# A second copy of the low part of k per head, so that both score products of a fused attention and convolution block contract over 128 rows

## The chip, the cores and the metric

The kernel runs on one core of a Trainium2 chip. The metric is the device time of one execution in microseconds (us), lower being better. TensorE does the matrix products, VectorE (DVE), ScalarE (ACT) and GpSimd (POOL) the rest, and SyncE (SP) issues nearly all DMA transfers, one after the other in program order.

## The reference

One encoder layer on 1024 tokens of 1024 channels. The input is normalised and multiplied by one wide matrix; its columns feed a convolution branch, an attention branch and a gate for each. The two results are joined, projected, added to the input and normalised again. The part that the change touches is the score of the neighbourhood attention, with 8 heads of 64 channels on a grid of 16 rows by 64 columns:

```
hn = rms_norm(h, ln_g[l])
proj = hn @ w_in[l] + b_in[l]
glu_a, glu_b, z_conv, q, k, v, z_att = jnp.split(proj, cuts, axis=-1)
...
# per row of the grid, window of 8 rows x 16 columns, clamped at borders
s = jnp.einsum("bhwd,bhiwjd->bhwij", q_row, k_win).astype(jnp.float32) * scale
s = s + bias
p = jax.nn.softmax(s.reshape(B, N_HEADS, GRID_W, kh * KW), axis=-1)
return jnp.einsum("bhwij,bhiwjd->bhwd", p, v_win)
```

## The kernel before

**Products in two parts.** Matrix products run in fp32r. To keep accuracy, each operand is split into a high part (the fp32r rounding) and a low part (what is left), and a product is the sum of high x high, low x high and high x low. A projection of 128 channels for 512 tokens is 24 matmuls of 512 columns (8 pieces of the contraction, three products each), in one PSUM bank.

**Scores.** Two heads make a pair, since 128 projected channels hold two heads. For a pair `i`, `query` and `kv` (with `q_out`, `k_out`, `v_out`) project q, k and v. For head `a` of the pair the tile `q[a]` holds 128 rows: the high part of q in 64 of them and its low part in the other 64. The tile `kh[a]` holds the high part of the head's k twice, in rows 0 to 63 and again in rows 64 to 127. So one matmul over 128 rows gives (q high + q low) x k high. The low part of k stands once per pair, in `kl`: 64 rows for each head. The second product, q high x k low, reads only the 64 rows of the head. A head is worked in 4 column blocks of 16 query columns; a block needs two score banks (`HF`, two halves of the query rows), each of one product with `kh` and one with `kl`, over 264 and 288 key columns (the two outer blocks) or 352 and 384 (the two inner ones). There are 32 blocks in all. I number them 0 to 31; blocks 0 to 3 are head 0, blocks 24 to 27 are head 6.

**A block's chain.** Scores (`s`, TensorE), minimum with the bias (`s<-s,bias`, DVE), exponential (`prob`, ACT), transposes (`ptp`, TensorE), high part (`pth`, ACT) and low part (`ptl`, DVE), product with v (`po<-pth,v` and `po<-ptl,v`, TensorE), copy (`os`, ACT), transpose back (`po<-ident,os`, TensorE), and `ytok` (ACT, then DVE). The scores of a block stand one block ahead of its transposes.

**What else runs beside it.** DVE does the depthwise convolution: 150 multiply-adds ("taps", `acc<-glu,dwc,acc`) that later feed a LayerNorm and a pointwise product (`ln`, `lnb`, `pw`, `yt`). TensorE fills the time between the steps of the chain with projections: `pq`, `pk`, `pv` of later pairs, `pz` of the gates. After these come the last gates and the output projection (`out`).

**What sets the order.** Every engine executes in program order. The program is written by a planner (class `Clock`): streams of work are woven together by an estimated clock of the engines, and a stream also waits for buffers. `r_u` counts 16 large buffers of 128x1024 fp32 (tag `u`): the tiles of x, of the convolution, of q, k and v, and others. `kv` takes 3 of them for k (two `kh`, one `kl`) and more for v; `scores` gives them back at the last block of a head. When a stream has to wait for a buffer, other work comes first, so a changed number of buffers changes the order on all engines.

**Copies between halves.** Channels of head 1 of a pair lie in rows 64 to 127, those of head 0 in rows 0 to 63. To have a part in both halves, `copy` moves 64 rows x 512 columns (128 KB) by a DMA on SP's queue. `k_out` does three for each half of the tokens: `kh[1]`'s rows of head 0 into both halves of `kh[0]`, and, when these are read, head 1's rows of `kh[1]` into its other half. The bias tiles of the following blocks (`bias<-row`, line 462) and the weights (`wr<-in_w_in`, line 213) go through the same queue.

Of the kernel before, what the change touches and what calls it, by code (L numbers as in the profile page):

```python
# [32 lines left out]
CH_A, CH_B, CH_ZC, CH_Q, CH_K, CH_V, CH_ZA = 0, 4, 8, 12, 16, 20, 24  # L33
# rows of the small-vector tile
V_LN, V_BIN, V_DWB, V_CLG, V_CLB, V_GNC, V_GNA, V_N = 0, 8, 36, 40, 44, 48, 52, 56
# column blocks of 16 queries: (first 8-column granule, granules, bias class)
BLK = [(0, 3, 0), (1, 4, 1), (3, 4, 1), (5, 3, 2)]
BW = [24, 32, 24]
# row halves: (first key row, key rows)
HF = [(0, 11), (4, 12)]  # L40
# [30 lines left out]
class Ring:  # L71
    """the buffers of a tag, by the time from which each is free"""

# [16 lines left out]
class Clock:  # L90
    """Every engine issues in the order of this program. The work comes as streams, generators that give the
    time from which they can go on; they are woven by a clock of the tensor engine and of the others' queues."""

# [55 lines left out]
def block(ctx: ExitStack, tc: tile.TileContext, x, vecs, w_in, dw_w, pw_w, pw_b, rpb, w_out, final_g, out):  # L149
# [41 lines left out]

# [1 line left out]
    warm = const.tile([P, 1], F32, name="warm")  # L193
# [4 lines left out]

# [1 line left out]
    acc = yp.tile([P, NC4, T], F32, name="acc")  # L200
# [4 lines left out]

    # chunks of the projection in the order of the work: glu, q, k and v, gates of the attention and of the convolution
    of = {"g": (CH_B, CH_A), "q": (CH_Q,), "k": (CH_K, CH_V), "a": (CH_ZA,), "c": (CH_ZC,), "p": ()}
# [73 lines left out]
    def turned(h):  # L281
        """first the banks of several chunks at a time, so that each tile of x is turned as it comes"""
        todo_ = list(range(NK))
        for group in ((("tr", "tr", "s", "s", "o", "ln"),) if h == 0 else ()) + (("tr",), ("s",)) * NK:
            ks, todo_ = todo_[:len(group)], todo_[len(group):]
            pts = []
            for k, tag in zip(ks, group):
                yield from RB[tag].get()
                pts.append((k, tag, bank(tag, f"px{h}_{k}", NB[tag])))
            for j in range(4):  # L290
                t = 4 * h + j
                while t not in x_ready:
                    yield ck.now + 0.1
                if x_ready[t] + ck.HOP > ck.now:
                    yield x_ready[t] + ck.HOP
                for k, tag, pt in pts:
                    ck.tp(pt[:, j * P:(j + 1) * P], xt[t][:, k * P:(k + 1) * P], ident)
                    if j == 3:
                        sl = slice(512 * h, 512 * h + 512)
                        e = ck.act(out=hi[k][:, sl], in_=pt, func=AF.Copy, scale=col(V_LN + k))  # L300
                        ck.spawn(low(h, k, pt, sl, e, RB[tag]), -1)
            yield
        for _ in range(4):
            r_u.put()
# [12 lines left out]
    bias = []  # L317
# [9 lines left out]

# [1 line left out]
    ready = {}  # L329

    def split(raw, whi, wlo, after=None, eng="pool"):
        """hi and lo of a weight; gives the time"""
        t = ck.act(after, out=whi, in_=raw, func=AF.Copy)
# [34 lines left out]
    def proj(w, h, name, order=None, tag="pj"):  # L368
        """one chunk of channels for half of the tokens; order: width of the column blocks
        that become the outer dimension of the tokens"""  # L370
        whi, wlo, wt = w
# [18 lines left out]

# [1 line left out]
    # CLS: first query row, first key row written, key rows, window by the row offsets -4..3  # L392
    CLS = ((0, 0, 8, False), (4, 0, 11, True), (8, 4, 12, True), (12, 8, 8, False))
# [3 lines left out]
    def bias_rows():  # L397
# [20 lines left out]
        r_gz.put()  # L418
        # a window that moves with the column: columns c0..c0+n, bias columns from 7 on
        for t, c0, n in ((0, 8, 8), (1, 0, 16), (2, 0, 9)):  # L420
            w = BW[t]
            for h in range(8):
# [3 lines left out]
                yield ck.now + 0.3  # L426
        # a window at the border
        for t, start, cs in ((0, 0, range(8)), (2, 8, range(9, 16))):
            for c in cs:
                nc.sync.dma_start(out=ab[t][:, c, :, start:start + 16], in_=rp8[:, :, 15 - c:31 - c])  # L430
                yield ck.now + 0.3
        # a row of mask before, and laid out for the query rows
        for t in range(3):
# [31 lines left out]

# [1 line left out]
    # a sigmoid is half of 1 + tanh of the half, and the taps carry the half  # L467
    u, conv_end = [], [0.0] * 8
# [21 lines left out]
    def all_taps():  # L490
        """two chunks in turn, so that a tap need not wait for the one before; the last chunk by halves of the tokens"""
        n = 0
# [45 lines left out]

# [1 line left out]
    pair = {}  # L540
# [16 lines left out]
    def kv(i):  # L557
        bk, bv = col(V_BIN + CH_K + i), col(V_BIN + CH_V + i)
        for _ in range(3):
            yield from r_u.get()  # L560
        wk = yield from weight(CH_K + i)
        kh = [U(f"kh{i}_{a}", F32R) for a in range(2)]
        kl = U(f"kl{i}", F32R)
        pair[i][1:3] = kh, kl
# [22 lines left out]
    def q_out(i, q, pq, sl, bq):  # L587
        """q[0]: hi and lo of the first head; q[1]: lo and hi of the second"""
        tag, r = (("gz", r_gz), ("ul", r_ul))[sl.start > 0]
# [17 lines left out]
    def k_out(i, kh, kl, pk, sl, bk):  # L607
        """kh[a]: hi of a head, twice; kl: lo of both"""
        t = ck.act(out=kh[1][:, sl], in_=pk, func=AF.Identity, bias=bk)
        yield t  # L610
        for half in (B, A):
            copy(kh[0][half, sl], kh[1][A, sl])
        t = ck.dve("scalar_tensor_tensor", t, out=kl[:, sl], in0=pk, scalar=bk, in1=kh[1][:, sl].bitcast(F32),
                   op0=ALU.add, op1=ALU.subtract)
        r_pj.put(t)
        yield max(t, ck.now + 2.8)
        pair[i][4][0].append(ck.now)
        copy(kh[1][A, sl], kh[1][B, sl])
        yield ck.now + 2.8
        pair[i][4][1].append(ck.now)  # L620
# [22 lines left out]
    def group_scale(src, ms, sq, sums=None):  # L643
        """ms: (mean of squares over each 64 + eps * sums^2) ** -0.5; sq is scratch"""
        g = sq.rearrange("p (g d) -> p g d", d=64)
# [12 lines left out]

# [1 line left out]
    def grid(ap):  # L660
# [5 lines left out]
    def scores(n):  # L666
        """S of a block of 16 columns of a head, and its exponentials"""
        i, a, b = blocks[n]
# [3 lines left out]
        head = 2 * i + a  # L672
        half = slice(64 * a, 64 * a + 64)
        khg, klg = grid(kh[a]), grid(kl)
        g0, ng, bt = BLK[b]
# [3 lines left out]
        for hf, (r0, nr) in enumerate(HF):  # L679
# [4 lines left out]
            ck.mm(so, q[a][:, qsl], khg[:, r0:r0 + nr, ks], True, False)  # L684
            ck.mm(so, q[a][half, qsl], klg[half, r0:r0 + nr, ks], False, True)
            sps.append(so)
        if b == 3:
            r_u.put()
            r_u.put()
            if a:  # L690
                r_u.put()
# [26 lines left out]
    def attention():  # L718
        """the scores run a block ahead"""
        yield from scores(0)  # L720
# [90 lines left out]

# [1 line left out]
    pwh, pwl, ln_end, stage = [], [], {}, [0]  # L813
# [22 lines left out]
    def pointwise(t):  # L836
# [35 lines left out]
        yield from r_ul.get()  # L872
        # half: z / 2; silu(z) = z / 2 * (1 + tanh(z / 2))
        th = half_tile("ul", f"th{t}")
# [39 lines left out]

# [1 line left out]
    def y_ready(c, h):  # L916
# [11 lines left out]
    def gated(y, pz, c, h, banks):  # L928
        """y: half of what z = pz + bias gates; silu(z) = z / 2 * (1 + tanh(z / 2))"""
        yield from r_gz.get()  # L930
# [21 lines left out]

# [1 line left out]
    def work(items):  # L954
# [73 lines left out]
    last = {}  # L1028
    # the chunks of the output projection that come last
    LATE = (3, 7)  # L1030
    K_OUT = [k for k in range(NK) if k not in LATE] + list(LATE)

    def final_gates():
        """the last two chunks of gates, k by k: each lets go of its part of the normalised input"""
        ends = (CH_ZC + 3, CH_ZA + 3)
# [27 lines left out]

# [1 line left out]
    def split_y(t):  # L1065
# [57 lines left out]
    def pieces(t):  # L1123
        """columns of the products of a tile; the last ones are short"""
        ends = (0, 512, 768, 1024) if t == NT - 1 else (0, 512, 1024)
        return [slice(a, b) for a, b in zip(ends, ends[1:])]
# [108 lines left out]
```

## Time and profile before

| what | value |
|---|---|
| median of 3 runs | 578.21 us (576.79 to 579.08) |
| span of the profiled execution | 576.6 us |
| TensorE busy | 557.6 us, 97% of the span, 2717 matmuls |
| TensorE's granted clock | 1.00 in nearly all of the span (mean 0.997) |
| DVE busy | 414.7 us, 72% |
| ACT, POOL busy | 259.7 us (45%), 191.7 us (33%) |
| chain that ended last | TensorE 82%, DVE 12% |

The span goes from the first to the last instruction of one profiled execution, and the profile gives no other time for that execution. The median of the runs is 1.6 us above the span. A TensorE that is "busy" may still be waiting inside: a matmul's duration holds the time in which it passes through the array, so durations of neighbours overlap. What tells more is the distance from one matmul's start to the next one's.

### The profile page before, as it was taken

The page shows a single profiled execution, that of the slowest core. Times are in us where ns is not written, and L with a number is a line of the kernel's source. Part 1 is how long each engine was busy: PE and PEld are TensorE (multiplying, and loading weights), DVE is VectorE, ACT ScalarE, POOL GpSimd, SP SyncE. Part 2 cuts the span into 40 slices and gives each one's busy share as a digit, 9 for nine tenths or more (in the row PEclk, how much of TensorE's full clock was granted, in tenths as well). Part 3 has the DMA queues.
Part 4 walks back from the last instruction along what each step waited for, and adds up shares of the span by engine and source line. Part 5 has one row for each costly group of instructions (what it writes and reads, how often), then busy time and mean ns, then how long its engine had stood idle before and what let it go on. Part 6 is the DMA issues. An engine that isn't in the chain of part 4 may idle for free.

```text
span 576.6 us, 7793 instructions
## 1 busy us (share of the span) xinstructions
PE 557.6 (97%) x2717; PEld 448.4 (78%) x2717; DVE 414.7 (72%) x665; ACT 259.7 (45%) x634; POOL 191.7 (33%) x176
## 2 busy tenths in 40 slices
PE   4999999899999999999999999999999999999995
PEld 3688887677878777777777877888888878888885
DVE  4747999999789988996899677756745265464232
ACT  5542221134554155544558455665755354253122
POOL 8413543241222331240524533642523353031121
PEclk9999999999999999999999999999999999999998
DMA  9413546652114422332232230120100580043221
GB/s 331 132 21 82 167 128 220 181 158 80 36 56 110 103 61 72 89 101 71 64 114 80 79 90 17 38 59 18 39 0 8 181 286 0 2 146 135 84 74 73
DMA packets 60410, 54.58 MB, mean 95 GB/s; under 512 B 9597, under 2 KB 51381, under 8 KB 60372
## 3 DMA queue, kind: packets, MB, share of 16 engines
q1 hardware_dynamic: 60302, 54.07, 31.0%
q8 instruction: 21, 0.34, 0.2%
q14 instruction: 17, 0.14, 0.1%
q10 hardware_dynamic: 70, 0.03, 0.0%
HBM read 36.58 MB, written 11.58 MB: 84 GB/s over the span
## 4 chain that ended last, share of the span: by engine, by line
PE 82%; DVE 12%; DMA 1%; ACT 1%; POOL 1%; SPq 1%; issue 1%; POOLq 0%; ACTq 0%; DVEq 0%
PE out L127 15%; PE pz L127 15%; DVE acc L140 10%; PE pv L127 8%; PE pk L127 7%; PE s L127 6%; PE pq L127 5%; PE ptp L131 5%; PE po L127 5%; PE pb L127 4%; PE pw L127 4%; PE pa L127 3%; PE po L131 1%; DMA x<-in_x 1%; PE px L131 1%; DVE x L140 1%
## 5 line engine op out<-in xcount | busy, mean ns | idle before, releaser
L140 DVE SCALAR_TENSOR_TENSOR acc<-glu,dwc,acc 128x512 f32<-128x512 f32 (+25 forms) x150 | 187.6, 1275 | 1.1
L144 POOL TENSOR_TENSOR wl<-wr,wh 128x512 fp32r<-128x512 f32 x56 | 89.1, 1610 | 133.1 <-ACT wh L136 127.9
L127 PE MATMUL pz<-hi,wh 128*128 128x512 f32 x128 | 52.3, 408 | 0.0
L127 PE MATMUL out<-wol,yh 128*128 128x512 f32 (+1 forms) x136 | 51.2, 377 | 0.0
L127 PE MATMUL out<-woh,yl 128*128 128x512 f32 (+1 forms) x136 | 51.2, 376 | 0.0
L127 PE MATMUL out<-woh,yh 128*128 128x512 f32 (+1 forms) x136 | 51.2, 376 | 0.0
L127 PE MATMUL pz<-hi,wl 128*128 128x512 f32 x128 | 50.3, 393 | 0.1
L127 PE MATMUL pz<-lo,wh 128*128 128x512 f32 x128 | 50.1, 391 | 0.0
L136 ACT ACTIVATE pth<-ptp 128x512 fp32r<-128x512 f32 x64 | 32.2, 544 | 32.2 <-PE ptp L131 32.2
L136 ACT ACTIVATE wh<-wr 128x512 fp32r<-128x512 f32 x56 | 32.3, 631 | 27.5 <-DMA wr<-in_w_in 14.2
L140 DVE TENSOR_TENSOR ptl<-ptp,pth 128x512 fp32r<-128x512 f32 x64 | 37.1, 614 | 1.7 <-ACT pth L136 1.3
L144 POOL TENSOR_TENSOR ams<-ams,mhalf 128x8 f32<-128x8 f32 x8 | 15.6, 1948 | 62.1 <-DVE ams L140 62.1
L140 DVE TENSOR_TENSOR xr<-out,xr 128x512 f32<-128x512 f32 (+1 forms) x17 | 11.1, 659 | 34.1 <-PE out L127 29.6
L136 ACT ACTIVATE prob<-s,mx 128x264 f32<-128x264 f32 (+1 forms) x64 | 33.7, 537 | 2.1 <-DVE mx L140 2.1
L131 PE MATMUL ptp<-ident,prob 128*128 128x128 f32 x224 | 32.0, 279 | 0.1
L140 DVE CUSTOM_DVE_ANT_0 s<-s,bias 128x264 f32<-128x264 f32 (+1 forms) x64 | 30.7, 507 | 1.6 <-PE s L127 0.7
L136 ACT ACTIVATE os<-po 128x256 f32<-128x256 f32 x32 | 12.4, 389 | 41.3 <-PE po L127 41.2
L127 PEld LDWEIGHTS out<-woh,yh 128*128 128x128 f32 x136 | 25.6, 188 | 4.8
L127 PEld LDWEIGHTS out<-woh,yl 128*128 128x128 f32 x136 | 25.6, 188 | 4.7
L127 PEld LDWEIGHTS out<-wol,yh 128*128 128x128 f32 x136 | 25.6, 188 | 4.6
L127 PE MATMUL po<-ptl,v 128*128 128x256 f32 x112 | 28.5, 284 | 0.5 <-DVE ptl L140 0.5
L131 PEld LDWEIGHTS ptp<-ident,prob 128*128 128x128 f32 x224 | 24.5, 140 | 5.7 <-issue 2.3
(153 smaller groups left out, 1380.7 us busy)
## 6 DMA issues: line engine op xcount, KB each, us to landing
wr<-in_w_in SPq DMA_DIRECT2D x28, 512.0 KB
x<-in_x SPq DMA_DIRECT2D x8, 512.0 KB
wor<-in_w_out SPq DMA_DIRECT2D x8, 512.0 KB
xr<-in_x SPq DMA_DIRECT2D x8, 512.0 KB
out<-xr SPq DMA_DIRECT2D x16, 256.0 KB
kh<-kh SPq DMA_DIRECT2D x24, 128.0 KB
q<-ql SPq DMA_DIRECT2D x16, 128.0 KB
row<-abn SPq DMA_DIRECT2D x16, 96.0 KB
```

Source lines behind the costliest of these rows:

```text
L127: self.nc.tensor.matmul(out, lhsT=lhsT, rhs=rhs, start=start, stop=stop)
L131: self.nc.tensor.transpose(out=out, in_=in_, identity=identity)
L136: self.nc.scalar.activation(**k)
L140: getattr(self.nc.vector, fn)(**k)
L144: getattr(self.nc.gpsimd, fn)(**k)
```

## The change

`kl` becomes two tiles of 128 rows, one per head, like `kh`: `kl[a]` has the low part of head `a`'s k in both halves. `k_out` writes the low parts of both heads into `kl[1]` as before (one DVE instruction) and copies: head 0's rows into both halves of `kl[0]`, then head 1's rows into the other half of `kl[1]`. That is 3 more copies for each half of the tokens, 24 in the kernel. `scores` uses all 128 rows for the second product too, which adds q low x k low to the sum. `kv` takes 4 buffers of `r_u` for k in place of 3, and each head gives back 3 at its last block (before: 2 at head 0, 3 at head 1).

```
     def kv(i):
         bk, bv = col(V_BIN + CH_K + i), col(V_BIN + CH_V + i)
-        for _ in range(3):
+        for _ in range(4):
             yield from r_u.get()
...
-        kl = U(f"kl{i}", F32R)
+        kl = [U(f"kl{i}_{a}", F32R) for a in range(2)]
...
     def k_out(i, kh, kl, pk, sl, bk):
...
         for half in (B, A):
             copy(kh[0][half, sl], kh[1][A, sl])
-        t = ck.dve("scalar_tensor_tensor", t, out=kl[:, sl], in0=pk, scalar=bk, in1=kh[1][:, sl].bitcast(F32),
+        t = ck.dve("scalar_tensor_tensor", t, out=kl[1][:, sl], in0=pk, scalar=bk, in1=kh[1][:, sl].bitcast(F32),
                    op0=ALU.add, op1=ALU.subtract)
         r_pj.put(t)
-        yield max(t, ck.now + 2.8)
+        yield t
+        for half in (B, A):
+            copy(kl[0][half, sl], kl[1][A, sl])
+        yield ck.now + 2.8
+        copy(kh[1][A, sl], kh[1][B, sl])
         pair[i][4][0].append(ck.now)
-        copy(kh[1][A, sl], kh[1][B, sl])
+        copy(kl[1][A, sl], kl[1][B, sl])
         yield ck.now + 2.8
         pair[i][4][1].append(ck.now)
...
     def scores(n):
...
-        half = slice(64 * a, 64 * a + 64)
-        khg, klg = grid(kh[a]), grid(kl)
+        khg, klg = grid(kh[a]), grid(kl[a])
...
             ck.mm(so, q[a][:, qsl], khg[:, r0:r0 + nr, ks], True, False)
-            ck.mm(so, q[a][half, qsl], klg[half, r0:r0 + nr, ks], False, True)
+            ck.mm(so, q[a][:, qsl], klg[:, r0:r0 + nr, ks], False, True)
             sps.append(so)
         if b == 3:
-            r_u.put()
-            r_u.put()
-            if a:
+            for _ in range(3):
                 r_u.put()
```

All engines keep their instructions apart from these copies, but the planner writes another order from the projections of pair 1 on. Three places matter below.

**SP's queue at the first pair**, between the first half's `kh` copies and the bias loads of the first blocks. Before:

```order
L585 DMA kh_0_935<-kh_1_936 64x512 x2
L448 DMA row_12_983<-abn_881 128x192 x2
L585 DMA kh_1_936<-kh_1_936 64x512
L462 DMA bias_0_147<-row_0_639 64x1x192
L462 DMA bias_0_147<-row_4_658 64x1x264
L585 DMA kh_0_935<-kh_1_936 64x512 x2
L462 DMA bias_1_148<-row_8_686 64x1x288
```

Now:

```order
L448 DMA row_12_984<-abn_881 128x192 x2
L585 DMA kl_0_937<-kl_1_938 64x512 x2
L462 DMA bias_0_147<-row_0_639 64x1x192
L585 DMA kh_1_936<-kh_1_936 64x512
L585 DMA kl_1_938<-kl_1_938 64x512
L462 DMA bias_0_147<-row_4_658 64x1x264
L585 DMA kh_0_935<-kh_1_936 64x512 x2
L462 DMA bias_1_148<-row_8_686 64x1x288
L585 DMA kl_0_937<-kl_1_938 64x512 x2
```

The second half's `kh` copies have three `kl` copies more ahead of them, and the second half's `kl_0` copies stand behind them, still ahead of the first block's last bias loads.

**TensorE in block 20** (head 5, first column block), between the transposes of the probabilities and the product with v. Before, the last transposes and the first of 18 `pk` matmuls; 12 `pw` matmuls follow these, and then `po_0`:

```order
L131 MATMUL ptp_0_2_3014<-ident,prob_0_153 128x128
L131 MATMUL ptp_0_2_3014<-ident,prob_0_155 128x128
L127 MATMUL pk_0_3023<-hi_131,wh_2860 128x512
L127 MATMUL pk_0_3023<-lo_139,wh_2860 128x512
L127 MATMUL pk_0_3023<-hi_131,wl_2861 128x512
```

Now, from the last transposes to the transpose back:

```order
L131 MATMUL ptp_0_2_2973<-ident,prob_0_155 128x128
L127 MATMUL pz_1_2905<-hi_138,wh_2655 128x512
L127 MATMUL pz_1_2905<-lo_146,wh_2655 128x512
L127 MATMUL pz_1_2905<-hi_138,wl_2656 128x512
L131 MATMUL ln_2998<-ident,acc 128x128 x4
L131 MATMUL ln_3010<-ident,acc 128x128 x4
L127 MATMUL po_0_2997<-pth_0_0_2970,v_1_2595 128x256
...
L127 MATMUL po_0_2997<-ptl_0_2_2977,v_1_2595 128x256
L131 MATMUL po_0_2997<-ident,os_0_3028 128x128 x2
```

30 large matmuls have become 3 and 8 small transposes, and nothing is left between the last `po_0` product and the transpose back. In block 21, just behind, 4 `lnb` transposes stand between `ptp` and `po_1`, and 4 between `po_1` and its transpose back; the `pk` of the last pair comes after that.

**TensorE in block 9** (head 2, second column block). Before, 3 `pq` matmuls stood between the last products with v and the transpose back; now none does:

```order
L127 MATMUL po_1_2098<-pth_1_2_2078,v_0_1934 128x256
L127 MATMUL po_1_2098<-ptl_1_2_2079,v_0_1934 128x256
L131 MATMUL po_1_2098<-ident,os_1_2109 128x128 x2
```

On DVE, 92 taps stand between the first score instruction of block 0 and that of block 24 before, and 102 now; the other 58 or 48 lie outside.

## Rows read from the trace of the kernel before

**Rows 1.** The page: busy time by engine, and the chain that ended last.

```profile
PE 557.6 (97%) x2717; PEld 448.4 (78%) x2717; DVE 414.7 (72%) x665; ACT 259.7 (45%) x634; POOL 191.7 (33%) x176
...
PE 82%; DVE 12%; DMA 1%; ACT 1%; POOL 1%; SPq 1%; issue 1%; POOLq 0%; ACTq 0%; DVEq 0%
```

**Rows 2.** Stretches: length, busy us of PE, PEld, DVE, ACT, POOL, clock, DMA, GB/s.

```profile
126.50:344.10 217.60, 217.03 (x1105) 170.60 (x1104) 186.91 (x320) 111.11 (x287) 63.89 (x44) 1.00 0.29 79
344.10:366.00 21.90, 21.90 (x108) 16.61 (x107) 18.45 (x39) 13.91 (x36) 11.48 (x9) 1.00 0.11 33
```

**Rows 3.** Instructions on the tile s: durations min/median/max, starts, forms.

```profile
L127 PE MATMUL s<-kh,q x64: 285/402/448, 126.5 to 433.5; 128*128 128x264 f32 x16, 128*128 128x288 f32 x16, 128*128 128x352 f32 x16, 128*128 128x384 f32 x16
...
L127 PE MATMUL s<-kl,q x64: 382/412/442, 126.7 to 433.9; 64*128 64x264 f32 x16, 64*128 64x288 f32 x16, 64*128 64x352 f32 x16, 64*128 64x384 f32 x16
```

**Rows 4.** Timeline of PE in blocks 11 and 14: start, duration, instruction.

```profile
229.86 0.37 PE L127 MATMUL s<-kh,q 128*128 128x264 f32 x1
...
231.13 0.66 PE L131 MATMUL ptp<-ident,prob 128*128 128x128 f32 x4
...
250.01 0.41 PE L127 MATMUL s<-kh,q 128*128 128x352 f32 x1
250.35 0.43 PE L127 MATMUL s<-kl,q 64*128 64x352 f32 x1
250.71 0.45 PE L127 MATMUL s<-kh,q 128*128 128x384 f32 x1
251.08 0.44 PE L127 MATMUL s<-kl,q 64*128 64x384 f32 x1
251.46 1.09 PE L131 MATMUL ptp<-ident,prob 128*128 128x128 f32 x8
```

**Rows 5.** Timeline of PE: products with v that follow one another.

```profile
254.83 0.28 PE L127 MATMUL po<-pth,v 128*128 128x256 f32 x1
254.95 0.28 PE L127 MATMUL po<-ptl,v 128*128 128x256 f32 x1
255.07 0.41 PE L127 MATMUL pv<-hi,wh 128*128 128x512 f32 x1
```

**Rows 6.** Timeline of PE's weight loads in block 14 and just after.

```profile
250.35 0.18 PEld L127 LDWEIGHTS s<-kl,q 64*128 64x128 f32 x1 [0.17 <-issue]
250.71 0.19 PEld L127 LDWEIGHTS s<-kh,q 128*128 128x128 f32 x1 [0.17 <-issue]
...
254.72 0.19 PEld L127 LDWEIGHTS po<-pth,v 128*128 128x128 f32 x1
```

**Rows 7.** Timeline around block 20, all engines: transposes, low part, product, copy, transpose.

```profile
313.29 0.88 PE L131 MATMUL ptp<-ident,prob 128*128 128x128 f32 x6
...
313.92 0.48 PE L127 MATMUL pk<-hi,wh 128*128 128x512 f32 x1
...
316.00 0.69 DVE L140 TENSOR_TENSOR ul<-xn,uh 128x512 fp32r<-128x512 f32 x1
...
316.61 1.01 DVE L140 TENSOR_TENSOR ptl<-ptp,pth 128x512 fp32r<-128x512 f32 x2
...
321.41 0.28 PE L127 MATMUL po<-ptl,v 128*128 128x256 f32 x1
...
322.23 0.38 PE L131 MATMUL po<-ident,os 128*128 128x128 f32 x2
```

**Rows 8.** Timeline of SP's queue at the first pair.

```profile
113.91 1.18 SPq L585 DMA_DIRECT2D kh<-kh  x2
115.83 0.82 SPq L448 DMA_DIRECT2D row<-abn  x2
118.37 0.47 SPq L585 DMA_DIRECT2D kh<-kh  x1
118.88 1.24 SPq L462 DMA_DIRECT2D bias<-row  x2
120.22 1.16 SPq L585 DMA_DIRECT2D kh<-kh  x2
```

**Rows 9.** DVE from 126.5 to 344.1: its longest waits, and a group of taps.

```profile
DVE ytok L140 <- ACT ytok L136: 15.6, 15, 2.6
...
L140 DVE SCALAR_TENSOR_TENSOR acc<-glu,dwc,acc 128x512 f32<-128x512 f32 x30 | 29.0, 968 | 0.4
```

## The prediction

> **What bounds the kernel now.** I read the page first: TensorE is busy for 97% of the span and makes up 82% of the chain that ended last, DVE 12% [rows 1]. Busy shares mix stages, so I cut the span where the scores run. From the first scores (126.5 us) to the first scores of block 24 (344.1 us), TensorE is busy for 217.03 of 217.60 us at a granted clock of 1.00, which is the upper of its two levels, 2.4 GHz, and DVE for 186.91 [rows 2]. So in that stretch TensorE sets the pace, and DVE has 30.7 us of idle time. From there to the end of the taps (366 us) TensorE is busy all the time, too. What the distance between TensorE's instructions costs in this stage is therefore paid in full.
>
> A busy TensorE can still be slow inside, so I read the timeline of single matmuls. Products with v, 256 columns each, start 0.12 us apart [rows 5], 0.47 ns a column. The scores don't run at this rate. Block 14 has two products of 352 and two of 384 columns; from the first one's start to the next work it takes 251.46 - 250.01 = 1.45 us. Block 11, with 264 and 288 columns, takes 231.13 - 229.86 = 1.27 us [rows 4]. The weight loads say why: the load of each product waits 0.17 us and begins only when the matmul before it is through, where the loads of the products with v overlap the running matmul [rows 6]. The loads that wait are those in which the number of rows changes, 128 to 64 and 64 to 128. It is not the accumulation into one bank: products with v accumulate likewise and don't wait, and the step from `kl` to the next bank's `kh` waits as well. The first transpose after the last `kl` product comes 0.38 us after that product's start [rows 4], late by the same amount.
>
> **The change, part by part.**
>
> *The row switches.* With 128 rows in both products I take the rate of the products with v: 2 x 552 columns x 0.47 ns = 0.52 us in place of 1.27, and 2 x 736 x 0.47 = 0.69 in place of 1.45. That saves 0.75 and 0.76 us. There are 16 blocks of each kind (64 products with `kh` and 64 with `kl`, each width 16 times) [rows 3]: 16 x 0.75 + 16 x 0.76 = 24.2 us. More rows don't lengthen a matmul: the `kh` products have 128, and no longer distance than the `kl` products. Bounds: nothing, if the wait has another cause; 24.2 us, if all of it goes. I take all, since every wait sits at a switch.
>
> By the Trainium skill ("TensorE: Matmul & The Clock Gate", section "Step-by-step: what each phase is for") a load is pulled ahead of running matmuls when the row groups don't conflict or when it goes to the background buffer, and the row count doesn't matter. By that the `kl` loads should have been hidden as the others are, and the sum would have 0 in place of 24.2. The trace speaks against it here, with 0.17 us of wait per load. A second page of the Trainium skill ("TensorEngine Tiling (Array Packing)", section "Key Properties") says that a change of the tiling mode drains the array, with which the trace agrees.
>
> *24 more copies.* DMA and SP have room in general; what counts is whether scores wait for a copy. At pair 0 they do. SP is free of the `row` copies at 116.65 us; a copy takes it up to 0.59 us, a bias load 0.62, and a copy that reads what an earlier one frees was issued 3.3 us after that one (115.09 to 118.37) [rows 8]. Going through the new queue: `kl_0` twice until 117.8, a bias load, `kh_1` until 118.9; `kl_1` must wait for `kl_0` until 121.1 and is out at 121.6; a bias load 122.2, `kh_0` twice 123.4, a bias load 124.0, `kl_0` twice 125.2. These land at about 128.5. The first `kl` product started at 126.7 [rows 3] and reads both halves of the tokens, so it comes 1.8 us later, and TensorE with it, because its projections stand behind. For the later pairs I take nothing: in the order, other matmuls stand between their k and their scores. Bounds: 0 (a landing that is faster than the wait shows) and 4 us (pair 1 late by as much).
>
> *The order.* The fourth buffer makes k of the last pair wait, and its projections no longer fill blocks 20 and 21. In block 20 of before, the last `ptl` ended at 317.62, 4.3 us after the first transpose began; `ul`, 0.61 us of that, isn't ahead of it any more, so 3.7 us [rows 7]. In the new order TensorE gets to the products that need it after 6 transposes (0.63), 3 `pz` (0.72), 8 transposes (0.84) and 4 products with v (0.48), 2.7 us: it waits 1.0. The transposes back come 322.23 - 321.41 = 0.82 us after the last product's start [rows 7], 0.12 without a wait: 0.7 more. Block 21 has 8 transposes, 4 `lnb` and 4 products in that place, 1.7 us, and a DVE queue of about the same length: 1.9 of wait, and 0.7 less the 4 `lnb` (0.4) behind it. Block 9 has nothing between product and transpose back: 0.7. Together 1.7 + 2.2 + 0.7 = 4.6 us. Bounds: 0 (if DVE and ACT run early) and twice that.
>
> *DVE.* A quicker TensorE leaves DVE less time for the same work, and the new order puts 10 more taps ahead of block 24, 0.97 us each [rows 9]. The stretch to block 24 becomes 217.6 - 24 x 0.755 + 1.8 + 4.6 = 205.9 us, and DVE needs 186.9 + 9.7 = 196.6 in it: 95%, where it had 86%. If all its idle time shrinks, this costs nothing. If all 30.7 us stay, the stretch is 227.3 and 21.4 us are lost. More than half of the idle time is DVE waiting for ACT's `ytok` (15.6 us in 15 waits) [rows 9], which hangs on TensorE's own product, so it shrinks when DVE comes later; DVE's low parts are needed soon after, and a late one stops TensorE. I take 4 us, nearer to the lower end.
>
> *The sum*, on the profiled execution's span: 576.6 - 24.2 + 1.8 + 4.6 + 4 = 562.8 us. The median of the runs is 1.6 us above the span, so 564 us.
>
> **The rivals.**
>
> 1. *All cover holds.* Waits in blocks 9, 20 and 21 vanish and DVE catches up: 576.6 - 24.2 + 1.8 + 1.6 = 556 us. For it: in 217.60 us TensorE lost almost nothing to waits for other engines [rows 2], so the chain's steps were early before. Against it: DVE at 95%.
>
> 2. *DVE becomes the bound* up to block 24. With three quarters of its idle time left (23 us) it costs 13.7, and the time is 574; with all of it 21.4, and 582, just slower than before. It decides against a gain when the stretch to block 24 isn't shorter than about 222 us. For it: TensorE's and DVE's work stand close together already, and both execute in a fixed order. Against it: what DVE waits for is mostly TensorE.
>
> 3. *The switch isn't the cause, and the time gets longer.* If a load of q's weights behind a score product waits whatever its rows are, nothing is saved, and the copies and the thinner order remain: 576.6 + 1.8 + 4.6 + 1.6 = 585 us. The place is every second load in a block; it decides as soon as less than 6.4 us of the 24.2 goes, a wait of 0.14 us or more left per product. For it: only score products show such waits at this size, and rows of before have no pair of score products over 128 rows. Against it: the transposes behind a `kl` product are late as well, and they load another weight. The pull-ahead rule of the Trainium skill named above would mean this case.
>
> **How the numbers follow.** My forecast, 558 to 572 us, has a chance of 0.60; all cover holding 0.21; DVE as the bound 0.13; no gain from the rows 0.06. The range from 554 to 576 us leaves out the slower part of the second rival, the third, and a little below: under 2 in 10. No change is within 0.5%, 575.3 to 581.1 us, about what a measurement of this kernel can tell. Faster: 0.60 + 0.21 and about 0.05 of the DVE case, less a little for the tail, 0.85. Same: 0.07, most of it DVE. Slower: 0.06 + 0.02 = 0.08.
>
> **What would show it.** In the profile after: start distances of the score matmuls of about 0.12 to 0.18 us, 0.5 to 0.7 us a block, and weight loads without a wait behind them; if the distances stay near 0.32 to 0.38, the step on the row switches is wrong. The first `kl` product near 128.5 us, or not. TensorE waits for `ptl` and `os` near blocks 9, 20 and 21. DVE nearly without idle time up to block 24, with TensorE waits for DVE spread over the blocks: more than 8 us of these, and the DVE step was too small. The forecast fails upward by DVE, and downward if the new order's thin places don't show.

## The result and the profile after

The changed kernel takes 572.32 us (median of 4 runs, 570.73 to 572.74); the kernel before, on the same chip, 578.22 us (4 runs, 576.79 to 579.08). The ratio is 0.9895, with an interval of 0.9870 to 0.9920: faster by 1.0%, 5.9 us, where the forecast was 14. The sign came as forecast. The time lies inside the range of 554 to 576 us, and 0.3 us above the 558 to 572 us that the forecast itself held likeliest. The gain is under half of the forecast one. The profiled execution has a span of 570.4 us.

The page of the changed kernel: busy time, and the chain that ended last.

```profile
PE 539.3 (95%) x2717; PEld 447.2 (78%) x2717; DVE 412.2 (72%) x665; ACT 260.1 (46%) x634; POOL 195.1 (34%) x176
...
PE 71%; DVE 17%; DMA 4%; issue 3%; ACT 2%; SPq 2%; POOL 1%; POOLq 0%; ACTq 0%; DVEq 0%
```

Against [rows 1], TensorE's share of the chain is down from 82 to 71%, and DVE, DMA and SP's queue have taken it over. So something was saved on TensorE, and something new is waited for.

**The saving** is seen in the group of the tile `s` (durations min/median/max, starts, forms) and in the timeline of block 13, matmuls first, weight loads below.

```profile
L127 PE MATMUL s<-kl,q x64: 280/323/495, 127.3 to 423.5; 128*128 128x264 f32 x16, 128*128 128x288 f32 x16, 128*128 128x352 f32 x16, 128*128 128x384 f32 x16
```

```profile
242.45 0.41 PE L127 MATMUL s<-kh,q 128*128 128x352 f32 x1
242.70 0.33 PE L127 MATMUL s<-kl,q 128*128 128x352 f32 x1
242.87 0.34 PE L127 MATMUL s<-kh,q 128*128 128x384 f32 x1
243.04 0.34 PE L127 MATMUL s<-kl,q 128*128 128x384 f32 x1
243.22 0.82 PE L131 MATMUL ptp<-ident,prob 128*128 128x128 f32 x6
```

```profile
242.53 0.19 PEld L127 LDWEIGHTS s<-kl,q 128*128 128x128 f32 x1
242.70 0.19 PEld L127 LDWEIGHTS s<-kh,q 128*128 128x128 f32 x1
```

The four products take 243.22 - 242.45 = 0.77 us, where block 14 of before took 1.45 [rows 4]. The load of each product now starts before the matmul ahead of it is through, with no wait noted [rows 6]. The second, third and fourth start 0.17 us apart, the rate of the products with v. Only the first is longer, 0.25 us, and it stands behind the small transposes back.

**What is waited for** stands in the list of TensorE's waits from 120 to 440 us (engine and line, waited for; total, times, longest). The same view of before has one row, 0.5 us for `ptl`.

```profile
PE pq L127 <- DVE v L140: 3.2, 2, 2.1
PE ln L131 <- DVE ptl L140: 2.9, 2, 2.3
PE s L127 <- ACT prob L136: 1.7, 1, 1.7
PE s L127 <- DMA kl<-kl: 1.4, 1, 1.4
PE po L131 <- ACT os L136: 1.2, 3, 0.5
```

Stretches (columns as in [rows 2]): the one from just before the first scores to just before block 24's, then the 3.4 us in which the granted clock is lower, twice.

```profile
125.00:343.90 218.90, 207.04 (x1113) 172.79 (x1112) 194.93 (x335) 110.45 (x284) 68.89 (x45) 0.98 0.36 95
...
134.50:137.90 3.40, 3.35 (x10) 2.90 (x11) 3.40 (x8) 1.86 (x6) 0.36 (x1) 0.50 0.66 192
...
308.60:312.00 3.40, 2.93 (x13) 2.63 (x12) 3.30 (x8) 2.02 (x6) 1.78 (x4) 0.50 0.00 0
```

TensorE, idle for 0.6 us of this part before, is idle for 11.9 now. And there are two stretches at a granted clock of 0.50, the lower level, 1.2 GHz. Each follows a series of waits; neither has a counterpart in [rows 2].

The first scores and block 24's start here:

```profile
125.62 0.29 PE L127 MATMUL s<-kh,q 128*128 128x264 f32 x1
...
344.51 0.37 PE L127 MATMUL s<-kh,q 128*128 128x264 f32 x1
```

That is 218.9 us, where before took 217.6 and the prediction's sum has 205.9, or 209.9 with its 4 us for DVE. Before's program has 9 `pv` matmuls fewer in this stretch, 2.1 us. So up to block 24 nearly all that the switches saved is lost again, and of the 8 us that the forecast missed, some 7 lie here.

**The first pair** (timeline, SP's queue and the scores; a bracket gives the wait and what ended it):

```profile
123.19 1.11 SPq L585 DMA_DIRECT2D kl<-kl  x2
124.41 0.53 SPq L213 DMA_DIRECT2D wr<-in_w_in  x1
124.98 1.32 SPq L462 DMA_DIRECT2D bias<-row  x2
...
127.32 0.36 PE L127 MATMUL s<-kl,q 128*128 128x264 f32 x1 [1.42 <-DMA kl<-kl]
...
127.72 0.44 DVE L140 CUSTOM_DVE_ANT_0 s<-s,bias 128x264 f32<-128x264 f32 x1 [1.52 <-PE s L127]
...
131.38 0.47 DVE L140 CUSTOM_DVE_ANT_0 s<-s,bias 128x288 f32<-128x288 f32 x1 [3.16 <-issue]
...
132.90 0.43 PE L127 MATMUL s<-kh,q 128*128 128x352 f32 x1 [1.73 <-ACT prob L136]
```

The first `kl` product waits for the last copies, as forecast. Then comes a second wait that was not forecast. The second part of the bias tile of the second score bank is loaded behind the `kl` copies, at 124.98, and DVE waits 3.16 us, until 131.38. The profile names no releaser here ("issue"); that DVE waits for the bias load is read from the program, and from e4_pool below, where the same instruction's wait is put down to it. So block 0's exponentials come late, its score banks come free late, and TensorE waits 1.73 us more before block 1's scores.

### The profile page after: what moved, and what is told of

It reads as the page before. It is cut to its first block, busy times and chain, and to the rows that moved or that the text cites. A ratio compares the mean times of both kernels' runs of the same rounds, so it can differ in the third digit from the quotient of the medians.

```text
span 570.4 us, 7827 instructions
## 1 busy us (share of the span) xinstructions
PE 539.3 (95%) x2717; PEld 447.2 (78%) x2717; DVE 412.2 (72%) x665; ACT 260.1 (46%) x634; POOL 195.1 (34%) x176
## 4 chain that ended last, share of the span: by engine, by line
PE 71%; DVE 17%; DMA 4%; issue 3%; ACT 2%; SPq 2%; POOL 1%; POOLq 0%; ACTq 0%; DVEq 0%
PE out L127 15%; PE pz L127 13%; DVE acc L140 12%; PE pv L127 6%; PE pk L127 6%; PE pq L127 5%; PE po L127 4%; PE pw L127 4%; PE pb L127 4%; PE ptp L131 3%; PE pa L127 3%; PE s L127 3%; DMA kl<-kl 1%; PE po L131 1%; DMA x<-in_x 1%
## 5 line engine op out<-in xcount | busy, mean ns | idle before, releaser
L144 POOL TENSOR_TENSOR wl<-wr,wh 128x512 fp32r<-128x512 f32 x56 | 93.9, 1695 | 153.0 <-ACT wh L136 147.7
L131 PE MATMUL ptp<-ident,prob 128*128 128x128 f32 x224 | 30.0, 273 | 0.0
L127 PE MATMUL pq<-hi,wh 128*128 128x512 f32 x64 | 26.6, 416 | 3.2 <-DVE v L140 3.2
L127 PE MATMUL po<-pth,v 128*128 128x256 f32 x112 | 29.5, 291 | 0.0
```

Of the source, the lines that this page charges most:

```text
L127: self.nc.tensor.matmul(out, lhsT=lhsT, rhs=rhs, start=start, stop=stop)
L131: self.nc.tensor.transpose(out=out, in_=in_, identity=identity)
L144: getattr(self.nc.gpsimd, fn)(**k)
```

## The experiments

The theory: the switch of rows is the cost, as forecast, and the new copies at the first pair and the new order each give a part of the gain back. Rival B: DVE is the bound up to block 24, so that a quicker TensorE can't show whatever the order is. Two kernels each do one half of the change, one does a milder form of it, and one moves the copies off SP's queue. All four ran beside the kernel before.

**e1_rows**: before, with the second product over all 128 rows of the pair's `kl`. This adds q low x the other head's k low to the sum. No copy, buffer or order changes.

```
-            ck.mm(so, q[a][half, qsl], klg[half, r0:r0 + nr, ks], False, True)
+            ck.mm(so, q[a][:, qsl], klg[:, r0:r0 + nr, ks], False, True)
```

> The kernel before with one edit: the second score product reads all 128 rows of the pair's kl tile and of q (which mixes in the other head's low part, so this part of the score is not the reference's). No copies, no fourth buffer, the order of before. Theory A (the row switches cost TensorE about 22 us, and the change gave most of it back in its copies and its order): 557 to 563 us, start distances of the score matmuls of 0.12 to 0.25 us, TensorE waits for DVE under 6 us. Theory B (DVE paces the stretch up to block 24, whatever the order): 570 to 574 us, like the changed kernel, with TensorE waits for DVE of 12 us and more. Theory C (the rows don't matter): 578 us and weight loads that still wait 0.17 us.

Measured: 558.86 us (5 runs) against 578.11; ratio 0.9654 (0.9633 to 0.9675), 19.3 us less. The same stretch as in [rows 2], and TensorE's waits from 120 to 440 us:

```profile
126.50:344.10 217.60, 214.42 (x1172) 179.66 (x1171) 196.19 (x349) 119.48 (x309) 69.56 (x49) 0.99 0.30 82
```

```profile
PE po L127 <- DVE ptl L140: 1.7, 1, 1.7
PE yt L131 <- POOL xn L144: 0.9, 1, 0.9
```

In the same 217.60 us TensorE issues 1172 matmuls instead of 1105, and it waits for DVE once for more than a microsecond. DVE is busy for 196.19 us, 90%, and keeps up. That refutes rival B. Added up over all 32 blocks, from each score product's start to the next instruction's, the scores took 43.1 us before and 22.4 here. The `ptp` transposes, the first of which also follows a switch, took 23.4 and 22.0. So the switches were worth 20.7 + 1.5 = 22.2 us, and 2.9 of that was lost again, mostly in these waits and in 3.4 us at the lower clock behind the first of them.

**e2_copies**: the change's copies, buffers and order, with the second product over 64 rows as before.

```
-            ck.mm(so, q[a][:, qsl], klg[:, r0:r0 + nr, ks], False, True)
+            ck.mm(so, q[a][half, qsl], klg[half, r0:r0 + nr, ks], False, True)
```

> The changed kernel, but the second product reads only the head's own 64 rows of kl[a], as before: the copies, the fourth buffer and the new order without the gain in rows. Theory A: 582 to 588 us, with waits of TensorE at the first scores (2 to 5 us) and near blocks 20 and 21 (3 to 6 us). Theory B: 577 to 580 us, since DVE needs its time either way and a slow TensorE hides the thin places. In both the weight loads of the scores wait 0.17 us.

Measured: 589.07 us (6 runs), ratio 1.0187 (1.0164 to 1.0209), 11.0 us more. TensorE's first waits of the same list:

```profile
PE pq L127 <- DVE v L140: 3.1, 2, 2.3
PE s L127 <- DMA kl<-kl: 1.8, 2, 1.5
```

The rest of the change costs 11 us alone, 1 us above the range of Theory A, and Theory B, by which it would have cost 2 us at most, is refuted. The two halves add up to -19.3 + 11.0 = -8.3, and the whole gives -5.9. The 2.4 us between them is about what two intervals leave open; if it is real, a slower TensorE hides some of these waits.

**e3_group**: before, with both products with `kh` of a block first and then both with `kl`, so that a block has two switches in place of four. It computes the same sums as before.

```
             ck.mm(so, q[a][:, qsl], khg[:, r0:r0 + nr, ks], True, False)
-            ck.mm(so, q[a][half, qsl], klg[half, r0:r0 + nr, ks], False, True)
             sps.append(so)
+        for hf, (r0, nr) in enumerate(HF):
+            qsl = slice(512 * hf + P * b, 512 * hf + P * b + P)
+            ck.mm(sps[hf], q[a][half, qsl], klg[half, r0:r0 + nr, ks], False, True)
```

> The kernel before with the four score products of a block in another order: both products with kh first, then both with kl over 64 rows. Two switches of the row count in a block in place of four, no copies, no buffer, nothing else moved. Theory A: half of the switches go, 64 x 0.17 = 11 us, so 566 to 569 us. Theory B: DVE paces, at most 6 us gained, 572 to 576. Theory C (a wait belongs to each load and not to the switch): 578 us.

Measured: 566.22 us (4 runs), ratio 0.9788 (0.9771 to 0.9804), 11.9 us less. An inner block on TensorE, and its weight loads:

```profile
244.16 0.58 PE L127 MATMUL s<-kh,q 128*128 128x352 f32 x2
244.67 0.61 PE L127 MATMUL s<-kl,q 64*128 64x352 f32 x2
245.21 1.09 PE L131 MATMUL ptp<-ident,prob 128*128 128x128 f32 x8
```

```profile
244.67 0.29 PEld L127 LDWEIGHTS s<-kl,q 64*128 64x128 f32 x2 [0.24 <-issue]
```

A block takes 245.21 - 244.16 = 1.05 us, between 1.45 and 0.77, and the first of its two `kl` loads is the one that waits. So the cost follows the number of switches, and not the number of products with 64 rows, which is unchanged. This kernel has no new copies, its TensorE waits for 2.0 us in all from 120 to 440 us, and it beats the change.

**e4_pool**: the change, with pair 0's `kl` copies issued by GpSimd.

```
-            copy(kl[0][half, sl], kl[1][A, sl])
+            copy(kl[0][half, sl], kl[1][A, sl], nc.gpsimd if i == 0 else None)
...
-        copy(kl[1][A, sl], kl[1][B, sl])
+        copy(kl[1][A, sl], kl[1][B, sl], nc.gpsimd if i == 0 else None)
```

> The changed kernel with the 6 copies of kl of the first pair issued by GpSimd in place of SP, so that the bias loads and the kh copies stand in SP's queue as before. Theory A (the first pair's copies hold the scores of blocks 0 and 1 up by 4 us, and TensorE's clock drops after it): the wait before block 1 goes, the one at block 0 shrinks, 567 to 570 us. Rival: the first scores wait for DVE's kl or the landing itself, not for SP's order: 571 to 573 us, the wait at block 0 as long as in the changed kernel.

Measured: 570.05 us (6 runs), ratio 0.9873 (0.9849 to 0.9896), which is not apart from the changed kernel's. SP's first two `kh` copies, the one that waits for them, and DVE's second score instruction:

```profile
113.35 1.18 SPq L585 DMA_DIRECT2D kh<-kh  x2
...
120.42 0.49 SPq L585 DMA_DIRECT2D kh<-kh  x1
...
130.70 0.47 DVE L140 CUSTOM_DVE_ANT_0 s<-s,bias 128x288 f32<-128x288 f32 x1 [2.27 <-DMA bias<-row]
```

Neither theory came out whole. The wait for the bias is over 0.7 us earlier, and still 2.27 us long; TensorE's wait before block 1's scores is 0.9 us in place of 1.7 and did not go, and the one at block 0 is 1.3 in place of 1.4. The copies are out of SP's queue, but the profile has them on another queue over the same 16 DMA engines, and the `kh` copy that must wait for the first two is issued 120.42 - 114.53 = 5.9 us after these, where it was 3.3 in before [rows 8]. So SP's order alone is not the cost. That landings got slower beside the added copies is read from this distance; how the cost divides between the two isn't shown.

Four more kernels ran, beside the kernel before again (577.63 us): the first separates the copies from the order, the others look into the order's waits.

**e5_order**: the change's program order on TensorE and DVE (four buffers counted, its yields), with the one tile per pair of e1_rows and without the new copies. Like e1_rows it adds q low x the other head's k low.

```
-        for _ in range(3):
+        for _ in range(4):
             yield from r_u.get()
...
-            ck.mm(so, q[a][half, qsl], klg[half, r0:r0 + nr, ks], False, True)
+            ck.mm(so, q[a][:, qsl], klg[:, r0:r0 + nr, ks], False, True)
```

> The order of the changed kernel without its copies: one kl tile for the pair, read over 128 rows (which mixes in the other head's low part), but four buffers counted for k and the same pauses, so that TensorE and DVE have the changed kernel's order. Theory A2 (the change lost about 13 us, of which some 5 by the copies at the first pair and 8 by the order): 565 to 568 us, no wait at blocks 0 and 1, the waits near blocks 8, 16, 20 and 21 as in the changed kernel. Rival (the copies cost nearly all of it, on the queue all along): 559 to 562 us. Rival (the order costs all of it): 571 to 573 us.

Measured: 566.06 us (5 runs), ratio 0.9797 (0.9772 to 0.9822), 11.6 us less. TensorE's waits, 120 to 440 us:

```profile
PE pq L127 <- DVE v L140: 3.2, 2, 2.1
PE ln L131 <- DVE ptl L140: 2.9, 2, 2.3
```

The waits for `v` and `ptl` of the changed kernel are all here, to the tenth of a microsecond. The two waits at the first pair are gone. So the order costs 19.3 - 11.6 = 7.7 us against e1_rows, and the copies cost 11.6 - 5.9 = 5.7 us. Each of these differences is known to about 2 us, from the intervals of two ratios.

All engines but for the copies execute the same instructions in the same order here as in the changed kernel, so the two traces can be laid side by side, matmul by matmul. The first `kl` product, block 1's first score and a `pb` matmul behind it, here:

```profile
125.74 0.28 PE L127 MATMUL s<-kl,q 128*128 128x264 f32 x1
...
129.34 0.33 PE L127 MATMUL s<-kh,q 128*128 128x352 f32 x1
...
132.08 0.39 PE L127 MATMUL pb<-lo,wh 128*128 128x512 f32 x1
```

In the changed kernel the same three start at 127.32, 132.90 and 138.19: 1.58, 3.56 and 6.11 us later. At the end it is 6.2. So in these traces the copies' whole price falls on the first pair, and the later pairs pay nothing.

**e6_taps**: the change, with every tap over half of its columns; half of the convolution is left out, and the order stays.

```
-            t = ck.dve("scalar_tensor_tensor", out=acc[:, j, t0:t1], in0=u[j][:, t0 + s:t1 + s],
-                       scalar=dwc[:, j, kk:kk + 1], in1=acc[:, j, t0:t1], op0=ALU.mult, op1=ALU.add)
+            m = t0 + (t1 - t0) // 2
+            nc.vector.scalar_tensor_tensor(out=acc[:, j, t0:m], in0=u[j][:, t0 + s:m + s],
+                                           scalar=dwc[:, j, kk:kk + 1], in1=acc[:, j, t0:m], op0=ALU.mult, op1=ALU.add)
```

> The changed kernel with every tap of the convolution over half of its columns (half of the convolution is left out), the order unchanged. Theory A2 (in the thin order, TensorE waits for v's low part before block 9's transposes and for ptl at block 20 because taps stand ahead of these on DVE): the waits before the first pq behind ptp (2.3 and 1.2 us) and before ln in block 20 (2.4 us) go or fall below 0.5 us, the lead before the first scores gets shorter by up to 3 us, and the waits for os and at blocks 0 and 1 stay; 560 to 567 us. Rival (it is the bare latency of the chain through ACT and DVE, whatever DVE has to do): the waits of 2.3, 1.2 and 2.4 us stay, and the time falls only by the lead, 568 to 571 us.

Measured: 560.39 us (4 runs), ratio 0.9702 (0.9679 to 0.9726). The wait for `v` at block 8:

```profile
212.34 0.47 PE L127 MATMUL pq<-hi,wh 128*128 128x512 f32 x1 [0.69 <-DVE v L140]
```

Of the gaps between TensorE's starts, the one at block 8 falls from 2.29 to 0.86 us, the one at block 16 from 1.23 to nothing, and block 20's from 2.44 to 1.40; a later one at block 21 grows to 1.99. No stretch at the lower clock is left. So DVE's queue of taps makes most of the waits at blocks 8 and 16 and somewhat under half of the one at block 20, which was expected to fall below 0.5; the rest is argued to be the length of the chain. Not all of the gain is theirs: the first scores come 2.4 us earlier, since taps stand ahead of them, too, and the waits at blocks 0 and 1, which were expected to stay, are 0.4 and 1.3 us in place of 1.4 and 1.7. At 144 us 6.0 of the 10.7 us between the two traces are there already, the stretch at the lower clock behind block 1 included.

**e8_fill**: the change, with one projection unit ahead of the last pair's k in the list of filling work.

```
-FILL = "g3 q1 k1 q2 k2 q3 a0 k3 a1 a2 c0 c1 c2".split()
+FILL = "g3 q1 k1 q2 k2 q3 a0 a1 k3 a2 c0 c1 c2".split()
```

> The changed kernel with one step moved in the list of fillers: the gate a1 ahead of k3, so that TensorE has a projection that needs no buffers while k of the last pair waits for its four. Theory A2 (the fourth buffer empties the filler around blocks 20 and 21, 5.7 us of waits and a drop of the clock of 1.7 us): those waits go, 564 to 567 us. Rival (DVE is behind there anyhow, and TensorE waits elsewhere for the same time): 570 to 573 us.

Measured: 567.06 us (4 runs), ratio 0.9820 (0.9795 to 0.9845), faster than the change by about 4 us. At block 20, TensorE has more `pz` matmuls to do:

```profile
306.14 1.09 PE L131 MATMUL ln<-ident,acc 128*128 128x128 f32 x8 [0.21 <-DVE ptl L140]
```

The wait for `ptl` is 0.21 us in place of 2.27, and there is no lower clock behind it (the stretch at the first pair remains); two smaller waits for GpSimd's `xn`, 1.8 us together, come later.

**e9_both**: e8_fill with e4_pool.

> The changed kernel with both repairs: a1 ahead of k3, and the first pair's copies of kl issued by GpSimd. Theory A2: the two gains add up, 562 to 565 us, which is still above the kernel that reads the pair's tile over 128 rows without any copy. Rival (they share one cause, DVE being late): no better than the better one of the two alone.

Measured: 565.61 us (5 runs), ratio 0.9802 (0.9775 to 0.9828), and no stretch at the lower clock. DVE's wait at the first pair, 122 to 134 us, is still there:

```profile
DVE s L140 <- DMA bias<-row: 2.2, 1, 2.2
```

This is 0.6 us above what was expected, and not apart from e8_fill alone, so that moving the copies to GpSimd gains time is shown by neither pair of kernels. With both mended, the change comes to where e3_group is without any new copy.

## Why the prediction was right in sign and wrong in size

Against the forecast's sum (-24.2 + 1.8 + 4.6 + 4 = -13.8 us), the runs give -22.2 for the switches, 2.9 + 7.7 = 10.6 for order and DVE together, and 5.7 for the copies: -5.9. So 2 of the missing 8 us were never there, 2 went to order and DVE, and 4, the largest part, to the copies.

**The step that failed most: 24 more copies, "I take nothing" beyond the landing.** It stopped at the landing of the last copies, and that part had the right size: the first `kl` product is 1.58 us late, where 1.8 was forecast (in part by luck, since it and the score before it both came about 1 us earlier than taken, at 127.3 and 125.6). That later pairs pay nothing was right, too. But the term of 1.8 is mis-sized: 5.7 in the runs, above its own upper bound of 4. What stands behind the copies in the same queue was not followed: [rows 8] showed the bias loads there, and DVE's second score instruction waits for one of them. e4_pool shows that the queue's order is not all of it. Against e5_order, the rest of the price is 1.9 us of TensorE waiting before block 1's scores, 0.7 before the `pvt` transposes behind them, and some 1.9 in and around the 3.4 us at the lower clock: with 1.58, 6.1 us.

**The row switches.** Mechanism right, size slightly off: 22.2 in place of 24.2 us. All waits of the loads went. The step took 0.12 to 0.18 us for each of the four products, but the first one, behind 128-column transposes, takes 0.25 (inner) and 0.21 (outer). The third rival is refuted by e1_rows. So is, here, the Trainium skill's rule ("TensorE: Matmul & The Clock Gate", section "Step-by-step: what each phase is for") taken as if it covered a change of rows: with it e1_rows should have gained nothing, and it gained 19.3 us. That is the prediction's reading of it: what the section says of the row count is about the time that a load takes, and there the traces agree, 0.18 us for 64 rows and 0.19 for 128 [rows 6]. The rule of "TensorEngine Tiling (Array Packing)", section "Key Properties", agrees with all runs, if a change of the row count is such a change of mode; it gives no price.

**The order.** Forecast 4.6 us at blocks 9, 20 and 21. Block 9 came out as worked out, 0.63 for 0.7: the timeline shows the wait behind the last product with v.

```profile
230.68 0.44 PE L131 MATMUL po<-ident,os 128*128 128x128 f32 x2 [0.47 <-ACT os L136]
```

Blocks 20 and 21 lost 5.4 us in gaps instead of 3.9, and another 1.2 by slower steps, nearly all of it at the lower clock: with block 9, 7.2 us for a term of 4.6. DVE's part was nearly as forecast: `ptl` ends at 307.83, 4.1 us after the first transpose, where 3.7 was taken. But the step let TensorE do 8 `ln` transposes in the meantime, and it could not, as the timeline shows:

```profile
303.77 0.82 PE L131 MATMUL ptp<-ident,prob 128*128 128x128 f32 x6
...
304.89 0.40 PE L127 MATMUL pz<-hi,wl 128*128 128x512 f32 x1
...
306.82 1.01 DVE L140 TENSOR_TENSOR ptl<-ptp,pth 128x512 fp32r<-128x512 f32 x2
...
307.56 1.09 PE L131 MATMUL ln<-ident,acc 128*128 128x128 f32 x8 [2.27 <-DVE ptl L140]
```

`ln` and `ptp` take turns in the same PSUM banks (tag `tr`), so `ln` must wait until `ptl` has read its bank. The wait comes 0.84 us of work earlier than forecast, and that work then stands behind it.

**DVE.** The term of 4 us was right as a size, and that was luck in part: its reason is one that the step named only in passing ("a late one stops TensorE"). DVE was not short of time. The step had it busy for 95% of a stretch of 205.9 us; it was busy for 194.93 of 218.90, 89%. It was late at single places, where the new order put taps ahead of a low part that TensorE's bank hung on. Block 8 is the largest:

```profile
215.77 3.98 DVE L140 SCALAR_TENSOR_TENSOR acc<-glu,dwc,acc 128x503 f32<-128x503 f32 x2
...
219.67 0.74 DVE L140 TENSOR_TENSOR v<-pvt,v 128x256 fp32r<-128x256 f32 x2
...
220.56 0.48 PE L127 MATMUL pq<-hi,wh 128*128 128x512 f32 x1 [2.12 <-DVE v L140]
```

The gaps of blocks 8 and 16 are 2.3 and 1.2 us, together 3.5. (With the 7.2 above that is 10.7 us read from the timeline, where the runs' differences give 10.6.) The second rival fell with e1_rows, and the first, that all cover holds, with these waits. (The second's limit of about 222 us for a gain is 217.6 + 8 x 0.755 = 223.6 by its own terms; nothing hangs on it.)

That the stretches at the lower clock come from the waits ahead of them is argued, not shown: e9_both and e6_taps, in which waits were shortened, have none, but e1_rows has one behind a single wait of 1.9 us, and no run changed the clock alone.

## What to carry to other kernels

When a transfer is added to a queue, price what stands behind it in that queue up to the next thing that an engine waits for, and what lands beside it, not only the transfer itself. When fill work is moved out of a chain, ask of each instruction that is to fill the gap instead whether its output bank is free by then. And where matmuls of different row counts alternate, try first to group them by row count: two switches less in each block gave 11.9 us here without any data moved, twice what the change gave.

## What the runs showed of the hardware

A switch between 64 and 128 rows costs TensorE (43.1 - 22.4 + 1.5) / 128 = 0.17 us, and with half as many switches (30.6 us of scores in e3_group, `ptp` as before) 9.7 / 64 = 0.15 us. With copies from GpSimd's queue under way beside them (e4_pool), two copies from one half of the partitions to the other let the copy that depends on them go after 5.9 us, in place of 3.3 in before. And a TensorE that is busy for 95% of the span can still fall to the lower clock, for 3.4 us at a time; in it, products with v start 0.21 to 0.23 us apart, in place of 0.12 [rows 5]:

```profile
309.06 0.41 PE L127 MATMUL po<-ptl,v 128*128 128x256 f32 x1
309.28 0.41 PE L127 MATMUL po<-pth,v 128*128 128x256 f32 x1
```
